# A two-layer hybrid block: the opening's loads, modulation and weight splits rearranged, with 18 unread matmuls on TensorE

## The chip, the core and the metric

The kernel runs on one core of one Trainium2 chip. The metric is the device time of one execution in microseconds (us). A core has five instruction streams that run side by side and wait for each other by semaphores: TensorE (PE in the profile; its weight loads are PEld), VectorE (DVE), ScalarE (ACT), GpSimd (POOL) and SyncE (SP). Each stream is strictly in order: an instruction that waits holds up everything behind it on its engine. In this kernel every load is issued by SP, so all loads stand in one queue.

## What is computed

Two layers of a flow-matching backbone act on 256 latent tokens (`x`) and 256 context tokens (`ctx`), 1024 features each, all in float32. Cut to the part that matters here, a layer begins like this:

```python
mod = (silu(c) @ w_mod[l] + b_mod[l])[:, None, :]
sh1, sc1, gt1, sh2, sc2, gt2 = split(mod, 6, axis=-1)
h = rms_norm(x, g_norm1[l]) * (1 + sc1) + sh1     # the same for ctx with c_ctx
z = h @ w_in[l]
...                                               # conv, Fourier, attention, gates, MLP
```

`z` feeds three mixers: a gated short convolution (columns B, C and X of `w_in`), a Fourier mixing (columns F) and attention (columns Q, K and V). Then come gates, projections and an MLP.

## The kernel before, in words

**Tiling.** Activations are kept feature-major: 8 feature tiles of 128 features, each with 512 tokens (two streams of 256). A product in near-float32 accuracy is three matmuls on split operands: high weight by high activation (L416), low weight by high activation (L419), high weight by low activation (L421). A weight chunk of 1024 rows by 256 columns is loaded as a raw tile; a "split" makes its high part by a cast on ScalarE (L356) and its low part by a subtraction on VectorE or GpSimd (L357).

**The opening** is all that stands before the first layer's other products. It needs `x` and `ctx` (1 MiB each; xraw), the shift and scale columns of `w_mod` (16 loads of 512 KiB, two for each feature tile; tiles `big`), and three chunks of `w_in` (F, C and X, each in two halves of 512 KiB: rows 0 to 511 for feature tiles 0 to 3, rows 512 to 1023 for tiles 4 to 7). Its steps:

- `turn_x` (L480, L484) transposes `x` on TensorE and copies it to xT; `spread_rows` gives 1/rms of each token to every partition.
- For each feature tile kt, `mod_start` multiplies the silu vector by that tile's shift and scale columns (L245, 16 matmuls that the trace records as 32), copies the sums (L252, DVE), transposes them (L254, PE) and adds the bias (L258, L262, DVE). `gain` is L231.
- `modulate` makes the normed tile: L209 (DVE), its high part L214 (ACT), its low part L201 (DVE).
- `go(kt)` runs the 18 matmuls of that feature tile: 6 for each of the chunks F, C, X.

The loop goes over kt = 0 to 7 and runs a tile's mod_start and modulate while TensorE does the products of the tile before. The chunks are split in whole halves of 1024 columns. Four of the six low parts are made by GpSimd: F's and C's first halves, C's and X's second halves.

**What follows** in the program: the product with chunk B (`convL_mm`, its raw tile `convL_raw`), the two Fourier products, then queries, keys and values. The raw tiles come from a pool of two buffers. F's raw tile (both halves) is the first, C's the second, and `convL_raw` takes the first again; its load can be issued when all that reads F's raw tile is done.

**What sets the order.** Program order is not the order on an engine: a scheduler moves instructions where it expects an engine to be free, save those held with `keep_in_program_order`. So work written later can stand early. Such work here: the rotary tables for attention (L648, L652 to L654 on DVE), 14 short instructions on `gqk`, `ropec` and `ropes`, whose six small loads (L594 to L598) stand on SP behind all 16 loads of `w_mod`.

Code lines that matter, as they are before:

```python
start_raw = [raw_tile(), raw_tile()]                 # F and C: the raw pool's two buffers
first_w = [Chunk(r, True, e) for r, e in zip(start_raw, ((G, V), (G, G), (V, G)))]
...
bch = None if last else plain(w_in[l], 0, OFF_B).prep()   # convL_raw: the first buffer again
```

Of the kernel before, what the change touches and what calls it, by code (L numbers as in the profile page):

```python
# [39 lines left out]
def hybrid_block_kernel(  # L40
# [197 lines left out]
    def mod_start(ft, parts, meanwhile):  # L238
        """Shift and scale of one feature tile, the sums over even and odd k side by side."""
        pb = pmod.tile([P, 2, P], F32, tag="mod", name=nm("mod"))  # L240
        ps, tp = pb[:, 0, :], pb[:, 1, :]
        for kt in range(KT):
            for i in range(2):
                g = 2 * i + kt % 2
                mm = PE.matmul(  # L245
                    ps[32 * g : 32 * g + 32, :], cT[:, kt, :], parts[:, i, kt, :],
                    start=kt < 2, stop=kt >= KT - 2,
                )
                if ft and kt == 0 and i == 0:
                    tc.keep_in_program_order(mm)  # L250
        sb = scratch()[:, :P]
        V.tensor_copy(sb, ps)  # L252
# [1 line left out]
        tc.keep_in_program_order(PE.transpose(tp, sb, ident))  # L254
        tv = tp.rearrange("p (g s) -> p g s", s=32)
        for i in (1, 0):
            m = modT[0][:, i * 8 + ft, :]
            V.tensor_tensor(  # L258
                m, tv[:, 2 * i, 0:2], prm[0][:, i * 8 + ft : i * 8 + ft + 1].to_broadcast([P, 2]),
                op=ALU.add,  # L260
            )
# [115 lines left out]

    def fetch(loads, nkt=8, eng=(V, V)):
        r = raw_tile()
        for dst, src in loads(r.rearrange("p (k n) -> p k n", n=256)):  # L380
            nc.sync.dma_start(dst, src)
# [60 lines left out]
    def start_mod(q):  # L442
        t = bigt([P, 2, 2, KT, P], F32)
        for f in range(2):
            for i in (1, 0):
                c0 = i * D + (2 * q + f) * P
                nc.sync.dma_start(  # L447
                    t[:, f, i], w_mod[0, :, c0 : c0 + P].rearrange("(k p) n -> p k n", p=P)
                )
                if (q, f, i) == (0, 0, 0):  # L450
                    start_weights(0)
        return t
# [38 lines left out]
    for l in range(DEPTH):  # L491
# [18 lines left out]
        if l == 0:  # L510
# [5 lines left out]
            first_w[0].prep(0)  # L516

            def between(kt):
                if kt > 1:
                    go(kt - 1, 0, 1)  # L520
                if kt == KT // 2:
                    first_w[1].prep(1)

            for kt in range(KT):
                mod_start(kt, sc0[kt // 2][:, kt % 2], lambda: between(kt))
                gn = gain(0, 1, 48, gn, kt, 1)
                modulate(hh, hl, [(kt, 0), (kt, 1)], rb, gn, sh1)
                if kt == 0:
                    for w in first_w[1:]:
                        w.prep(0)  # L530
# [1 line left out]
                    go(0, 0, 1)
                if kt:
                    go(kt - 1, 1, 3)
                if kt in (2, 4):
                    first_w[kt - 2].prep(1)
# [546 lines left out]
```

## Time and profile before

| | |
|---|---|
| time, median of 3 runs | 1157.92 us (1157.07 to 1158.3) |
| span of the profiled execution, first to last instruction | 1156.9 us |
| mean granted TensorE clock over the span | 0.997 |
| bytes read from HBM | 177.81 MB |

The profiled execution has no time of its own on the page beside its span; the timed runs lie 0.2 to 1.4 us above that span, so about 1 us lies around it.

How to read the rows below: the timeline gives start, duration, engine, line, operation, output<-inputs with shapes, the count of merged instructions, and in brackets the idle time of the engine just before, with what ended it. A `SPq` row is SP issuing a load, not the load itself. The table by windows gives for each stretch its length, then busy time and instruction count of each engine, the granted TensorE clock, the busy share of the DMA engines (it can exceed 1) and GB/s.

### The profile page before, as it was taken

The numbers are of one execution on the slowest core, as the hardware profiler recorded it, in microseconds if no ns is written. First come the engines' busy times: TensorE is split into PE (matmuls) and PEld (weight loads), VectorE is DVE, ScalarE is ACT, GpSimd is POOL, SyncE is SP. The second block draws the span as 40 slices with busy tenths as digits, with TensorE's granted clock in tenths as the row PEclk, the third lists the DMA queues.
The fourth block names the chain that finished last, engine by engine and source line by source line (L and its number), as shares of the span: only waits on it lengthen the run. The fifth ranks groups of instructions, "written<-read, shape, count | busy, mean of one in ns | idle before, by whom it ended". The sixth has DMA issues, their size and how long they took to land.

```text
span 1156.9 us, 18548 instructions
## 1 busy us (share of the span) xinstructions
PE 1134.0 (98%) x7451; PEld 1001.1 (87%) x7451; DVE 781.5 (68%) x1446; ACT 501.3 (43%) x890; POOL 59.3 (5%) x57
## 2 busy tenths in 40 slices
PE   6899999999999999999999999999999999999998
PEld 4689987887787998878888888899999999999998
DVE  4677775567879785776746664678876567755754
ACT  4244444434332454144234135244666456744641
POOL 2102100000000100000000000043300000000000
PEclk9999999999999999999999999999999999999999
DMA  9923222234656253555455664515434465555552
GB/s 289 288 80 107 92 91 92 83 90 120 192 167 189 77 175 129 185 181 180 134 176 199 212 211 150 188 63 182 129 129 127 123 209 172 197 183 176 189 187 81
DMA packets 165743, 180.06 MB, mean 156 GB/s; under 512 B 5245, under 2 KB 144153, under 8 KB 165657
## 3 DMA queue, kind: packets, MB, share of 16 engines
q1 hardware_dynamic: 165656, 178.88, 49.1%
q8 instruction: 58, 0.95, 0.3%
q14 instruction: 29, 0.23, 0.1%
HBM read 177.81 MB, written 1.05 MB: 155 GB/s over the span
## 4 chain that ended last, share of the span: by engine, by line
PE 90%; SPq 3%; DMA 3%; DVE 2%; ACT 1%; POOL 0%; issue 0%; DVEq 0%; ACTq 0%
PE ffL_mm L416 15%; PE ffL_mm L419 14%; PE ffL_mm L421 14%; PE gateL_mm L416 5%; PE gateL_mm L419 5%; PE gateL_mm L421 5%; PE agL_mm L416 3%; PE agL_mm L419 3%; PE agL_mm L421 3%; SPq L447 2%; PE woL_mm L419 2%; PE woL_mm L421 2%; PE woL_mm L416 2%; PE gateL_aux L796 2%; PE gateL_aux L771 2%; PE qkvL_mm L748 2%
## 5 line engine op out<-in xcount | busy, mean ns | idle before, releaser
L356 ACT CAST ffL_whi<-ffL_raw 128x1024 fp32r<-128x1024 f32 x128 | 134.2, 1050 | 223.5 <-PE ffL_mm L421 211.4
L357 DVE TENSOR_TENSOR ffL_wlo<-ffL_raw,ffL_whi 128x1024 fp32r<-128x1024 f32 x127 | 155.2, 1223 | 102.7 <-ACT ffL_whi L356 102.6
L416 PE MATMUL ffL_mm<-ffL_big,ffL_whi 128*128 128x256 f32 (+1 forms) x544 | 173.3, 329 | 0.3 <-DVE xT L434 0.3
L419 PE MATMUL ffL_mm<-ffL_big,ffL_wlo 128*128 128x256 f32 (+1 forms) x544 | 172.3, 327 | 0.0
L416 PE MATMUL ffL_mm<-woL_big,ffL_whi 128*128 128x258 f32 (+2 forms) x544 | 171.2, 328 | 0.0
L419 PE MATMUL ffL_mm<-woL_big,ffL_wlo 128*128 128x258 f32 (+2 forms) x544 | 170.8, 327 | 0.0
L421 PE MATMUL ffL_mm<-ffL_big,ffL_whi 128*128 128x256 f32 (+1 forms) x544 | 137.9, 327 | 0.0
L421 PE MATMUL ffL_mm<-woL_big,ffL_whi 128*128 128x258 f32 (+2 forms) x544 | 134.0, 328 | 0.0
L416 PEld LDWEIGHTS ffL_mm<-ffL_big,ffL_whi 128*128 128x128 f32 x544 | 103.4, 190 | 11.0 <-issue 2.5
L416 PEld LDWEIGHTS ffL_mm<-woL_big,ffL_whi 128*128 128x128 f32 x544 | 102.7, 189 | 10.2 <-issue 1.6
L419 PEld LDWEIGHTS ffL_mm<-ffL_big,ffL_wlo 128*128 128x128 f32 x544 | 103.4, 190 | 9.0 <-issue 0.4
L419 PEld LDWEIGHTS ffL_mm<-woL_big,ffL_wlo 128*128 128x128 f32 x544 | 102.9, 190 | 8.9 <-issue 0.4
L323 DVE SCALAR_TENSOR_TENSOR ffL_acc<-ffL_modr,cs,ffL_acc 128x512 f32<-128x512 f32 x126 | 90.4, 747 | 25.9 <-DMA ffL_modr<-in_w_mod_dram 24.8
L421 PEld LDWEIGHTS ffL_mm<-ffL_big,ffL_whi 128*128 128x128 f32 x544 | 93.6, 190 | 8.6
L421 PEld LDWEIGHTS ffL_mm<-woL_big,ffL_whi 128*128 128x128 f32 x544 | 91.2, 189 | 8.7
L357 DVE TENSOR_TENSOR gateL_wlo<-gateL_raw,gateL_whi 128x1024 fp32r<-128x1024 f32 x40 | 48.9, 1222 | 13.4 <-ACT gateL_whi L356 13.3
L356 ACT CAST gateL_whi<-gateL_raw 128x1024 fp32r<-128x1024 f32 x40 | 42.0, 1050 | 26.9 <-PE gateL_mm L421 20.7
L774 DVE TENSOR_REDUCE gateL_mx<-gateL_aux 128x1 f32<-128x512 f32 (+1 forms) x48 | 28.7, 600 | 34.5 <-PE gateL_aux L771 34.2
L434 DVE SCALAR_TENSOR_TENSOR xT<-ffL_mm,modT,xT 128x256 f32<-128x256 f32 x80 | 34.1, 478 | 25.3 <-PE ffL_mm L421 25.2
L416 PE MATMUL gateL_mm<-n1L_big,gateL_whi 128*128 128x512 f32 x128 | 50.8, 398 | 0.0
L419 PE MATMUL gateL_mm<-n1L_big,gateL_wlo 128*128 128x512 f32 x128 | 50.8, 397 | 0.0
L419 PE MATMUL woL_mm<-agL_big,woL_wlo 128*128 128x256 f32 (+1 forms) x160 | 47.4, 307 | 0.0
(325 smaller groups left out, 2447.6 us busy)
## 6 DMA issues: line engine op xcount, KB each, us to landing
ffL_raw<-in_w_ff_dram SPq DMA_DIRECT2D x64, 1024.0 KB, 5.2
ffL_modr<-in_w_mod_dram SPq DMA_DIRECT2D x53, 512.0 KB, 5.6
gateL_raw<-in_w_in_dram SPq DMA_DIRECT2D x16, 1024.0 KB, 7.1
init_big<-in_w_mod_dram SPq DMA_DIRECT2D x16, 512.0 KB, 7.6
agL_raw<-in_w_in_dram SPq DMA_DIRECT2D x8, 1024.0 KB, 5.2
woL_raw<-in_w_o_dram SPq DMA_DIRECT2D x8, 1024.0 KB
qkvL_raw<-in_w_in_dram SPq DMA_DIRECT2D x6, 1024.0 KB
agL_modr<-in_w_mod_dram SPq DMA_DIRECT2D x11, 512.0 KB, 3.6
```

Source lines behind the costliest of these rows:

```text
L323: v = V.scalar_tensor_tensor(a, r[:, kk, :], w, a, op0=ALU.mult, op1=ALU.add)
L356: a = A.copy(hi[:, :n], src)
L357: b = eng.tensor_tensor(lo[:, :n], src, hi[:, :n].bitcast(F32), op=ALU.subtract)
L416: m = PE.matmul(d, wh, rh, start=kt == first, stop=False)
L419: PE.matmul(d, wl, rh, start=False, stop=False)
L421: PE.matmul(d, wh, rl, start=False, stop=kt == final)
L434: V.scalar_tensor_tensor(xT[:, f, cs], ps[:, cs], gt[:, f, s : s + 1], xT[:, f, cs], op0=ALU.mult, op1=ALU.add,)
L447: nc.sync.dma_start(t[:, f, i], w_mod[0, :, c0 : c0 + P].rearrange("(k p) n -> p k n", p=P))
L748: PE.matmul(ps, a, wh, start=kt == 0, stop=False)
L771: PE.matmul(sc, qT[:, h, q0 : q0 + P], kT[:, h // 4, e, ks], start=e == 0, stop=e == 1)
L774: V.reduce_max(mx, sc, axis=AX.X, negate=True)
L796: PE.matmul(yp[g * HD : (g + 1) * HD, :], vt[:, k0 + kk, g * HD : (g + 1) * HD], pts[g][:, kk, :], start=kk == 0, stop=kk == nk - 1,)
```

## The change

Five things are changed, all in the opening of layer 0.

1. **Loads.** The two loads of `w_mod` for feature tile 0 and the bias rows now stand ahead of `x` on SP; `x` and `ctx` come in four loads in place of two; the second halves of the `w_in` chunks come after tile 5's `w_mod` columns instead of after tile 3's.
2. **Tile 0's shift and scale** are computed ahead of the transposes of `x`.
3. **No split on GpSimd.** The low parts are made on VectorE, and each chunk is split in slices, one feature tile at a time (`Sliced.part`), so the raw tiles of F, C and X are read until the slice of tile 7 is made.
4. **Grouping.** Tiles 4 and 5 share one mod_start with 256 columns.
5. **18 unread matmuls** (`warm`): three times six matmuls of two constant tiles, before the first transposes, after the first transposes of `x`, and before the first products.

```diff
+W_INIT, W_X, W_RMS = 6, 6, 6
...
+    sc0 = [bigt([P, 2, 2, KT, P], F32)]
+    start_mod(sc0[0], 0)
+    load_rows(0)
     for i, src in enumerate((x[0], ctx_in[0])):
-        nc.sync.dma_start(xraw[:, i], src.rearrange("(t p) d -> p t d", p=P))
-    load_rows(0)
+        for tt in range(2):
+            nc.sync.dma_start(xraw[:, i, tt], src[tt * P : (tt + 1) * P, :])
...
+    def warm(n):
+        ps = pmod.tile([P, P], F32, tag="mod", name=nm("mod"))
+        for _ in range(n):
+            tc.keep_in_program_order(PE.matmul(ps, ones, ident, start=True, stop=True))
...
+    class Sliced(Chunk):
+        def part(self, k0, k1):
+            i = k0 // 4
+            if i not in self.pieces:
+                self.pieces[i] = [wpool.tile([P, 1024], F32R, tag=t, name=nm(t))
+                                  for t in ("whi", "wlo")]
+            hi, lo = self.pieces[i]
+            c = slice((k0 - 4 * i) * 256, (k1 - 4 * i) * 256)
+            tc.keep_in_program_order(A.copy(hi[:, c], self.raws[i][:, c]))
+            tc.keep_in_program_order(V.tensor_tensor(
+                lo[:, c], self.raws[i][:, c], hi[:, c].bitcast(F32), op=ALU.subtract))
...
-    first_w = [Chunk(r, True, e) for r, e in zip(start_raw, ((G, V), (G, G), (V, G)))]
+    start_weights(0)
+    for f in range(1, KT):
...
+        start_mod(sc0[f // 2], f)
+        if f == 5:
+            start_weights(1)
+    first_w = [Sliced(r) for r in start_raw]
+
+    mod_start(0, sc0[0][:, 0:1], lambda: None)
+    gn = gain(0, 1, 48, None, 0, 1)
...
+            groups = [(0,), (1,), (2,), (3,), (4, 5), (6,), (7,)]
+            due = []
+            for n, fts in enumerate(groups):
+                while len(due) > 1:
+                    go(due.pop(0))
...
+                if n == 1:
+                    go(0, 0, 2)
+                if n:
+                    mod_start(f0, sc0[f0 // 2][:, f0 % 2 : f0 % 2 + nf],
+                              lambda: n == 1 or go(due[0], 0, 1))
+                    gn = gain(0, 1, 48, gn, f0, nf)
+                else:
+                    first_w[0].part(0, 1)
+                modulate(hh, hl, [(f, s) for f in fts for s in range(2)], rb, gn, sh1)
+                for w in first_w[not n :]:
+                    w.part(f0, f0 + nf)
+                if n == 0:
+                    turn_x(range(NT0, KT))
+                else:
+                    go(due.pop(0), cut, 3)
+                due += fts
```

In the lists below a row is line, operation, output<-inputs (with buffer numbers) and size; line numbers are those of each kernel's own file, and the changed kernel's are higher: L201, L209, L252 and L357 are L220, L228, L270 and L410 there, L416, L419 and L421 are L451, L454 and L456.

**VectorE, where the rotary tables stand.** Before, they follow the low part of feature tile 5 (L201), and the next copy for a mod_start (L252, tile 6) stands among them:

```order
L201 SCALAR_TENSOR_TENSOR n1L_big_189<-n1L_scr_473,modT_120,n1L_big_188 128x256
L648 TENSOR_SCALAR gqk<-gqk 128x64
L652 TENSOR_TENSOR qkvL_tc_118_885<-ropec,gqk 128x64
L653 TENSOR_TENSOR qkvL_ts_119_886<-ropes,gqk 128x32
L652 TENSOR_TENSOR qkvL_tc_116_877<-ropec,gqk 128x64
L653 TENSOR_TENSOR qkvL_ts_117_878<-ropes,gqk 128x32
L654 TENSOR_TENSOR qkvL_ts_117_878<-ropes,gqk 128x32
L252 COPY n1L_scr_511<-n1L_mod_494 128x128
```

After, on the same engine: the tables (L682 and L686 to L688) stand among the low parts of tiles 4 and 5, and ahead of all three slices of F, C and X for these tiles (L410; `n1L_wlo_521` is F's). Nine more of the table rows, like those shown, stand where the line of dots is.

```order
L228 SCALAR_TENSOR_TENSOR n1L_scr_515<-xT,init_gain_186,init_aux_221 128x256
L682 TENSOR_SCALAR gqk<-gqk 128x64
L686 TENSOR_TENSOR qkvL_tc_119_914<-ropec,gqk 128x64
L687 TENSOR_TENSOR qkvL_ts_120_915<-ropes,gqk 128x32
L688 TENSOR_TENSOR qkvL_ts_120_915<-ropes,gqk 128x32
L220 SCALAR_TENSOR_TENSOR n1L_big_238<-n1L_scr_511,modT_132,n1L_big_237 128x256
...
L688 TENSOR_TENSOR qkvL_ts_118_907<-ropes,gqk 128x32
L220 SCALAR_TENSOR_TENSOR n1L_big_238<-n1L_scr_515,modT_132,n1L_big_237 128x256
L410 TENSOR_TENSOR n1L_wlo_521<-init_raw_135,n1L_whi_520 128x512
L410 TENSOR_TENSOR n1L_wlo_525<-init_raw_136,n1L_whi_524 128x512
L410 TENSOR_TENSOR n1L_wlo_529<-init_modr_138,n1L_whi_528 128x512
```

What moved: before, all low weights of these tiles were made elsewhere or earlier, and a copy for mod_start waited behind the tables; after, the low weights of tiles 4 and 5 wait behind them.

**VectorE, at the opening's end.** After, the last reader of F's raw tile (`init_raw_135`) is the slice for tile 7, behind that tile's low parts:

```order
L228 SCALAR_TENSOR_TENSOR n1L_scr_653<-xT,init_gain_186,init_aux_221 128x256
L220 SCALAR_TENSOR_TENSOR n1L_big_238<-n1L_scr_650,modT_132,n1L_big_237 128x256
L220 SCALAR_TENSOR_TENSOR n1L_big_238<-n1L_scr_653,modT_132,n1L_big_237 128x256
L410 TENSOR_TENSOR n1L_wlo_521<-init_raw_135,n1L_whi_520 128x256
L410 TENSOR_TENSOR n1L_wlo_525<-init_raw_136,n1L_whi_524 128x256
L410 TENSOR_TENSOR n1L_wlo_529<-init_modr_138,n1L_whi_528 128x256
L464 TENSOR_TENSOR uL_big_694<-n1L_mm_239,uL_big_694 128x512
```

Before, the last VectorE reader of that tile (`init_raw_123` there) is the whole half for tiles 4 to 7, which stands behind tile 2's low parts and ahead of tile 3's copy:

```order
L201 SCALAR_TENSOR_TENSOR n1L_big_189<-n1L_scr_360,modT_120,n1L_big_188 128x256
L201 SCALAR_TENSOR_TENSOR n1L_big_189<-n1L_scr_363,modT_120,n1L_big_188 128x256
L357 TENSOR_TENSOR n1L_wlo_381<-init_raw_123,n1L_whi_380 128x1024
L252 COPY n1L_scr_401<-n1L_mod_384 128x128
L258 TENSOR_TENSOR modT_120<-n1L_mod_384,prm_110 128x2
```

What moved: the last read of F's raw tile goes from tile 2's place to tile 7's.

**SP, the load queue.** After (before, the rows from `ropec` to `convL_raw` stand in the same order, at the same place behind all sixteen loads of `w_mod`):

```order
L484 DMA init_raw_135<-in_w_in_dram 128x4x256
L484 DMA init_raw_136<-in_w_in_dram 128x4x256
L484 DMA init_modr_138<-in_w_in_dram 128x4x256
L115 DMA init_big_157<-in_w_mod_dram 128x8x128 x4
L628 DMA ropec<-in_rope_c_dram 128x2x64
L629 DMA ropes<-in_rope_s_dram 128x2x64
L631 DMA gqk<-in_g_q_dram 128x64
L632 DMA gqk<-in_g_k_dram 128x64
L631 DMA gqk<-in_g_q_dram 128x64
L632 DMA gqk<-in_g_k_dram 128x64
L291 DMA gateL_modr_1512<-in_w_mod_dram 128x2x512
L416 DMA convL_raw_737<-in_w_in_dram 128x8x256
```

What did not move: the tables' loads and `convL_raw`'s stay behind the same bytes. Further on, from the middle of layer 0's queries and keys to the end, the order on all engines is that of before, row by row.

More of the change, by code (lines that the diff above doesn't have):

```diff
@@ L109, in hybrid_block_kernel, with start_mod @@
     xraw = bigt([P, 2, 2, D], F32)
+    def start_mod(t, f):
+        for i in (1, 0):
+            c0 = i * D + f * P
+            nc.sync.dma_start(
+                t[:, f % 2, i], w_mod[0, :, c0 : c0 + P].rearrange("(k p) n -> p k n", p=P)
+            )
+    sc0 = [bigt([P, 2, 2, KT, P], F32)]
+    start_mod(sc0[0], 0)
+    load_rows(0)
     for i, src in enumerate((x[0], ctx_in[0])):
-        nc.sync.dma_start(xraw[:, i], src.rearrange("(t p) d -> p t d", p=P))
-    load_rows(0)
+        for tt in range(2):
+            nc.sync.dma_start(xraw[:, i, tt], src[tt * P : (tt + 1) * P, :])
     ident = const.tile([P, P], F32, tag="ident", name="ident")
@@ L122, in hybrid_block_kernel @@
     cs2 = const.tile([P, 2, KT], F32, tag="cs2", name="cs2")
+    def warm(n):
+        ps = pmod.tile([P, P], F32, tag="mod", name=nm("mod"))
+        for _ in range(n):
+            tc.keep_in_program_order(PE.matmul(ps, ones, ident, start=True, stop=True))
+    warm(W_INIT)
     prm = []
@@ L236, in gain, with mod_start @@
         return g
-    def mod_start(ft, parts, meanwhile):
-        pb = pmod.tile([P, 2, P], F32, tag="mod", name=nm("mod"))
-        ps, tp = pb[:, 0, :], pb[:, 1, :]
+    def mod_start(f0, parts, meanwhile):
+        n = parts.shape[1]
+        pb = pmod.tile([P, 2, n, P], F32, tag="mod", name=nm("mod"))
+        ps, tp = pb[:, 0], pb[:, 1]
         for kt in range(KT):
@@ L244, in mod_start @@
                 g = 2 * i + kt % 2
-                mm = PE.matmul(
-                    ps[32 * g : 32 * g + 32, :], cT[:, kt, :], parts[:, i, kt, :],
+                tc.keep_in_program_order(PE.matmul(
+                    ps[32 * g : 32 * g + 32], cT[:, kt, :], parts[:, :, i, kt, :],
                     start=kt < 2, stop=kt >= KT - 2,
[L248 to L252, printed above, removed]
+                ))
+        sb = scratch((P, 4, P))[:, :n]
+        tc.keep_in_program_order(V.tensor_copy(sb, ps))
         meanwhile()
-        tc.keep_in_program_order(PE.transpose(tp, sb, ident))
-        tv = tp.rearrange("p (g s) -> p g s", s=32)
+        for f in range(n):
+            tc.keep_in_program_order(PE.transpose(tp[:, f], sb[:, f], ident))
+        tv = tp.rearrange("p f (g s) -> p f g s", s=32)
         for i in (1, 0):
-            m = modT[0][:, i * 8 + ft, :]
-            V.tensor_tensor(
-                m, tv[:, 2 * i, 0:2], prm[0][:, i * 8 + ft : i * 8 + ft + 1].to_broadcast([P, 2]),
+            a = i * 8 + f0
+            m = modT[0][:, a : a + n, :]
+            tc.keep_in_program_order(V.tensor_tensor(
+                m, tv[:, :, 2 * i, 0:2], prm[0][:, a : a + n].unsqueeze(2).to_broadcast([P, n, 2]),
                 op=ALU.add,
-            )
-            V.tensor_tensor(m, tv[:, 2 * i + 1, 0:2], m, op=ALU.add)
+            ))
+            tc.keep_in_program_order(
+                V.tensor_tensor(m, tv[:, :, 2 * i + 1, 0:2], m, op=ALU.add))
     def mod_loads(todo):
@@ L439, in residual @@
                 acc[s].add(f)
[L442 to L452, printed above, removed]
     start_raw = [raw_tile(), raw_tile()]
@@ L464, in start_weights @@
             )
-    sc0 = [start_mod(0), start_mod(1)]
-    start_weights(1)
-    sc0 += [start_mod(2), start_mod(3)]
-    first_w = [Chunk(r, True, e) for r, e in zip(start_raw, ((G, V), (G, G), (V, G)))]
+    start_weights(0)
+    for f in range(1, KT):
+        if f % 2 == 0:
+            sc0.append(bigt([P, 2, 2, KT, P], F32))
+        start_mod(sc0[f // 2], f)
[4 more added lines that the diff above has]
+    gn = gain(0, 1, 48, None, 0, 1)
     ss0 = small([P, 4], "ss")
@@ L486, in hybrid_block_kernel @@
     turn_x(range(NT0))
+    warm(W_X)
     rb0 = spread_rows(ss0, 4)
+    warm(W_RMS)
     rb = [rb0[:, s * S : (s + 1) * S] for s in range(2)]
@@ L502, in hybrid_block_kernel @@
             hh, hl = bigt([P, KT, 512]), bigt([P, KT, 512])
-            gn = None
         else:
@@ L514, in go @@
                 fm(first_w[a:b], hsrc, (0, T), banks[2 * a : 2 * b], (kt,), 0, 7, True)
[L516 to L530, printed above, removed]
-                    turn_x(range(NT0, KT))
[L532 to L536, printed above, removed]
+            groups = [(0,), (1,), (2,), (3,), (4, 5), (6,), (7,)]
[3 more added lines that the diff above has]
+                    go(due.pop(0))
+                f0, nf = fts[0], len(fts)
+                cut = 2 if n == 1 else 1
+                if n == 1:
[10 more added lines that the diff above has]
+                if n == 0:
+                    turn_x(range(NT0, KT))
+                else:
+                    go(due.pop(0), cut, 3)
+                due += fts
             for i in range(3):
```

1 line of the change is left out of this document (added).

## The prediction

> **What bounds the kernel now.** First the page, then the table by windows, cut at TensorE's restarts.
>
> ```profile
> span 1156.9 us, 18548 instructions
> PE 1134.0 (98%) x7451; PEld 1001.1 (87%) x7451; DVE 781.5 (68%) x1446; ACT 501.3 (43%) x890; POOL 59.3 (5%) x57
> ```
>
> ```profile
> core 0: us, PE busy (x) PEld busy (x) DVE busy (x) ACT busy (x) POOL busy (x), PEclk, DMA share, GB/s
> 0.00:20.19 20.19, 9.47 (x75) 8.06 (x75) 7.50 (x24) 10.01 (x18) 4.63 (x12) 1.00 0.93 286
> 4.00:44.00 40.00, 32.52 (x278) 25.50 (x278) 21.15 (x62) 16.00 (x28) 7.05 (x4) 0.96 1.11 314
> 20.19:23.05 2.86, 2.86 (x6) 1.83 (x6) 1.46 (x3) 1.83 (x2) 1.90 (x1) 0.50 1.16 291
> 46.48:50.37 3.89, 0.74 (x3) 0.31 (x4) 2.53 (x10) 0.00 (x0) 1.14 (x1) 1.00 0.71 159
> 50.37:54.97 4.60, 4.60 (x14) 3.37 (x14) 3.03 (x17) 0.91 (x2) 0.00 (x0) 0.63 1.03 348
> 54.97:69.89 14.92, 14.92 (x122) 11.91 (x122) 8.32 (x24) 5.62 (x10) 0.27 (x4) 1.00 0.17 61
> 69.89:110.00 40.11, 40.11 (x294) 38.16 (x293) 30.26 (x74) 18.37 (x39) 4.87 (x6) 1.00 0.41 133
> 110.00:1150.00 1040.00, 1035.22 (x6687) 917.50 (x6686) 711.74 (x1257) 457.87 (x810) 42.27 (x33) 1.00 0.48 152
> ```
>
> TensorE is the bound from 54.97 on: no idle time to 110, and 4.78 us of it in the 1040 us after. So what the opening gains or loses reaches the end nearly one for one, and the change has to be read in the first 70 us. There TensorE starts products at 20.19 (at a granted clock of 0.50), stands still for 3.15 of the 3.89 us after 46.48, and runs at 0.63 behind that. The DMA engines are full from 4 to 44 us. What ends the middle stall is in the timeline:
>
> ```profile
> 42.70 2.41 POOL L357 TENSOR_TENSOR n1L_wlo<-init_raw,n1L_whi 128x1024 fp32r<-128x1024 f32 x1 [19.18 <-ACT n1L_whi L356]
> 43.27 4.63 DVE L201 SCALAR_TENSOR_TENSOR n1L_big<-n1L_scr,modT,n1L_big 128x256 fp32r<-128x256 f32 x2 [0.19 <-ACT n1L_big L214]
> ...
> 45.19 0.47 SPq L597 DMA_DIRECT2D gqk<-in_g_q_dram  x1
> ...
> 49.26 0.20 DVE L648 TENSOR_SCALAR gqk<-gqk 128x64 f32<-128x64 f32 x1 [1.36 <-DMA gqk<-in_g_q_dram]
> ...
> 50.03 0.28 DVE L252 COPY n1L_scr<-n1L_mod 128x128 f32<-128x128 f32 x1
> 50.23 0.21 DVE L652 TENSOR_TENSOR qkvL_tc<-ropec,gqk 128x64 f32<-128x64 f32 x1
> ...
> 50.37 0.33 PE L254 MATMUL n1L_mod<-ident,n1L_scr 128*128 128x128 f32 x1 [1.68 <-DVE n1L_scr L252]
> ...
> 51.11 0.15 DVE L258 TENSOR_TENSOR modT<-n1L_mod,prm 128x2 f32<-128x2 f32 x1
> ```
>
> Two things delay VectorE here. Two low parts (L201) take 4.63 us while GpSimd splits weights; then the rotary tables wait for `gqk`, whose load SP issues only at 45.19, behind the sixteen `w_mod` loads. The second ends last: 49.26 us, which I call T.
>
> **The change, part by part.**
>
> *Start.* Tile 0's shift and scale leave the path behind `x`, warm matmuls run in TensorE's idle time (the first window has 10.72 us of it), and GpSimd's splits go. All that can bring: the slow clock of the first six products (2.86 us at half clock, so 1.4), perhaps 1 us of an earlier start (x lands later by the 1 MiB put ahead of it, but the chain behind it is shorter; bounds minus 1 to plus 2), and 3.75 us of VectorE (4.63 against 0.88 for two L201 without GpSimd, row below). None of it reaches the end, since TensorE then runs into the next wait sooner: it would finish tile 3's products near 43, and VectorE reach the tables near 44 (20.2 less 1, less 1.4 of slow clock, plus four tiles of 5.5 us, and 2 for the doubled mod_start).
>
> The rule on this: the Trainium skill, TensorE: Matmul & The Clock Gate, "What's actually happening", says that half clock is the default after an idle window of about 3.4 us and full clock returns after about as much work. By it the warm matmuls save the 1.4 us, and a wait of less than 3.4 us further on costs no clock, which would make my sum below 1.2 us smaller (1164.8). The trace is harsher: idle stretches of 1.48 and 1.68 us with 0.74 us of work between were followed by a clock of 0.63.
>
> *The tables' wait.* The order on VectorE puts the tables ahead of all three low slices of tiles 4 and 5, without which `go(4)` stops at its second matmul. Their loads stand behind the same bytes as before, and the loads fill the DMA engines (314 GB/s from 4 to 44), so T stays 49.26 (bounds: minus 1 if the pieces of `x` flow better, plus 1 if `w_mod` at the head starts the flow later). Prices:
>
> ```profile
> 32.33 0.88 DVE L201 SCALAR_TENSOR_TENSOR n1L_big<-n1L_scr,modT,n1L_big 128x256 fp32r<-128x256 f32 x2 [0.19 <-ACT n1L_big L214]
> 33.67 1.23 DVE L357 TENSOR_TENSOR n1L_wlo<-init_raw,n1L_whi 128x1024 fp32r<-128x1024 f32 x1 [0.46 <-ACT n1L_whi L356]
> ...
> 54.97 1.08 PE L245 MATMUL n1L_mod<-init_big,init_scr 128*32 128x128 f32 x32
> ...
> 60.46 1.08 PE L245 MATMUL n1L_mod<-init_big,init_scr 128*32 128x128 f32 x32
> ...
> 64.92 0.89 DVE L201 SCALAR_TENSOR_TENSOR n1L_big<-n1L_scr,modT,n1L_big 128x256 fp32r<-128x256 f32 x2 [0.19 <-ACT n1L_big L214]
> ...
> 65.81 0.39 PE L416 MATMUL n1L_mm<-n1L_big,n1L_whi 128*128 128x512 f32 x1
> ...
> 69.89 0.39 PE L416 MATMUL convL_mm<-n1L_big,convL_whi 128*128 128x512 f32 x1
> 70.93 0.42 DVE L357 TENSOR_TENSOR fouL_wlo<-fouL_raw,fouL_whi 128x256 fp32r<-128x256 f32 x1
> ```
>
> After T, VectorE does 14 table rows (before: 49.26 to 51.11 with one L252 of 0.20 from start to start among them, so 1.65), two L220 (0.88) and F's slice of 512 columns (between 0.42 for 256 and 1.23 for 1024: 0.69). TensorE restarts at 49.26 + 3.22 = **52.5**, where it restarted at 50.37. Left then: 17 matmuls of `go(4)` (18 take 65.81 to 69.89, 4.08, so 3.9), plus 1.7 of slow clock (in 50.37 to 54.97 it lost 37% of 4.60), to mod_start(6) at 58.1; one tile period (54.97 to 60.46, 5.49) to mod_start(7) at 63.6; and as before 9.43 from there (60.46 to 69.89). The opening ends at 73.0 against 69.89: **plus 3.1**.
>
> *The load of `convL_raw`.* Before, F's raw tile was free after 33.67, and the load was issued long before use. Now its last reader is the slice of tile 7.
>
> ```profile
> 48.53 0.38 SPq L381 DMA_DIRECT2D convL_raw<-in_w_in_dram  x1
> ...
> 56.39 1.05 ACT L356 CAST convL_whi<-convL_raw 128x1024 fp32r<-128x1024 f32 x1 [3.28 <-DMA convL_raw<-in_w_in_dram]
> ...
> 70.45 0.37 SPq L381 DMA_DIRECT2D qkvL_raw<-in_w_in_dram  x1
> ...
> 75.92 1.05 ACT L356 CAST qkvL_whi<-qkvL_raw 128x1024 fp32r<-128x1024 f32 x1 [4.53 <-DMA qkvL_raw<-in_w_in_dram]
> 77.01 1.23 DVE L357 TENSOR_TENSOR qkvL_wlo<-qkvL_raw,qkvL_whi 128x1024 fp32r<-128x1024 f32 x1 [0.28 <-ACT qkvL_whi L356]
> ```
>
> Tile 7's low parts end 5.35 us after its L245 (65.81 less 60.46); with F's slice (0.42) the buffer is free at 63.6 + 5.8 = 69.4. SP is idle then and issues. The price of such a load in an empty queue is `qkvL_raw`'s: cast 5.47 after the issue, high part ready at 6.5, low part at 7.79 (78.24 less 70.45). So the high part is there at 75.95 and the low part at 77.2, while TensorE is done at 73.0. Behind the waiting load on SP stand `fouL_raw`, a `modr` load and layer 1's rows; TensorE needs none of them for another 5 us. Two matmuls run on the high part alone (0.45), so the stretch counts as started at 76.75; after 2.95 us idle the clock is slow again, as behind the 3.15 us before. It lasts some 3.6 us, of which 2.4 fall behind 77.2, and costs 1.2. The product with B stands where it would after a start at 77.95: 4.95 behind the opening's end. Bounds: the waiting load lands up to 1 us sooner or later, and the clock costs 0 to 1.8; 2.8 to 6.5.
>
> *Sum.* 77.95 less 69.89 is plus 8.06. The profiled execution goes from 1156.9 to 1165.0 in span; with about 1 us around it, as the runs have (median 1157.92), **1166.0 us**. Later slices, SP's order and GpSimd's other splits are as before, so nothing gives it back beyond part of the 4.78 us of idle time after 110.
>
> **The rivals.**
>
> *The B load is hidden* (its buffer is free earlier than I read, or the load is quicker than 3 us): only the 3.1 is left, 1161.0. For it: the buffers are given out by a pool that I read in the code, not in a trace. Against it: the load writes the whole raw tile, and the order shows a reader of that tile at tile 7.
>
> *The queue runs faster*, the one mechanism that ends on the other side. Place: SP's loads ahead of `gqk` and `convL_raw`. If the tables land before VectorE reaches them near 44, the restart is at 44 + 3.2 and the 8.1 falls by 5.3; if the 1 MiB load also takes 3 us in place of 5.47, it falls by 2.5 more, to plus 0.3: 1158.2. It decides when T is under 44 and the load under 5. Against it: 314 GB/s with full engines over 40 us, and the same bytes ahead of the tables (13.6 MB for the 13 MiB of `x`, `w_mod` and `w_in`: 43 us at that rate, from about 3.5).
>
> *GpSimd was the bound*: if the 4.63 us row made the whole stall, its end returns 3.15 idle and 1.7 of slow clock: 1153.0. For it: the first idle stretch, 1.48 us, is ended by that L201. Against it: behind it, VectorE still waits 1.36 us for `gqk`, and new work stands behind that wait. The Trainium skill, SBUF — State Buffer, "Who interferes with whom", says that a VectorE instruction with two SBUF inputs contends with a GpSimd instruction that reads SBUF; by that rule the removal frees VectorE at once. The trace agrees (4.63 against 0.88), but the rule says nothing of the wait behind it.
>
> *Later still*: T moves by 1 or more, or the conv and Fourier stretch finds another late load: 1169.
>
> That the change does not do what it says (warm matmuls that leave the clock at half) would cost 1.4 us ahead of the tables' wait and change nothing behind it.
>
> **How the numbers follow.** Forecast 0.72 (1166.0, own range 1163.5 to 1168); B load hidden 0.10 (1161.0); faster queue 0.06 (1158.2); GpSimd 0.06 (1153.0); later 0.06 (1169). The measurement can tell about 0.2% here, 2.3 us. Faster 0.06; same 0.06; slower 0.88. The range takes the forecast and the hidden load and leaves out both lower cases and most of the later one: 1160.5 to 1168.5.
>
> **What would show it.** In the profile after: VectorE idle until `gqk` near 49 with TensorE idle from about 43 to 52.5; products at half clock behind; no GpSimd split in the opening and two low parts in 0.9 us; SP idle until near 69, then `convL_raw`; TensorE idle for about 3 us ahead of the first `convL_mm`, near 76, and a first pause behind its first two matmuls. Wrong, if the tables start without a wait, or `convL_raw` is issued near 48 as before.

## The result and the profile after

| | before | after |
|---|---|---|
| time, median | 1157.57 us (1157.07 to 1158.3) | 1165.36 us (1164.99 to 1166.6) |
| ratio | | 1.0073, 95% interval 1.0061 to 1.0085 (the two medians alone give 1.0067) |
| span of the profiled execution | 1156.9 us | 1163.7 us (its time: 1165.53) |

The changed kernel is slower by 0.7%. The table by windows of the kernel after, cut at TensorE's restarts as it was for before (length, then busy time and count for each engine, granted TensorE clock, DMA share, GB/s):

```profile
0.00:19.81 19.81, 14.62 (x111) 13.46 (x111) 6.78 (x25) 9.71 (x18) 2.28 (x11) 1.00 0.94 295
19.81:22.76 2.95, 2.95 (x12) 2.17 (x12) 1.14 (x4) 0.55 (x2) 0.00 (x0) 1.00 1.14 288
45.90:52.10 6.20, 0.00 (x1) 0.01 (x1) 3.19 (x18) 0.49 (x1) 0.00 (x0) 0.69 0.52 144
52.10:57.60 5.50, 5.50 (x17) 4.19 (x17) 1.15 (x2) 0.00 (x0) 0.00 (x0) 0.73 0.01 3
57.60:72.79 15.19, 15.19 (x121) 11.65 (x120) 8.50 (x28) 5.79 (x14) 0.27 (x4) 1.00 0.20 61
72.79:83.05 10.26, 7.48 (x20) 5.46 (x20) 8.64 (x12) 3.25 (x4) 0.00 (x0) 0.67 0.76 251
110.00:1150.00 1040.00, 1036.85 (x6706) 919.31 (x6706) 717.87 (x1274) 462.71 (x824) 44.68 (x35) 1.00 0.48 152
```

The start is better than before: products begin at 19.81 at full clock (before: at 20.19, at half clock), and GpSimd (the fifth pair) splits nothing. Then TensorE stands still for 6.20 us ahead of 52.10, and for 2.78 of the 10.26 us behind 72.79, with a slow clock after both. In the long stretch from 110 on it idles 3.15 us (before: 4.78).

The timeline of the kernel after at the first of these places:

```profile
45.41 0.49 PE L451 MATMUL n1L_mm<-n1L_big,n1L_whi 128*128 128x512 f32 x1 [1.69 <-ACT n1L_whi L409]
48.83 0.20 DVE L682 TENSOR_SCALAR gqk<-gqk 128x64 f32<-128x64 f32 x1 [4.53 <-DMA gqk<-in_g_q_dram]
51.36 1.28 DVE L410 TENSOR_TENSOR n1L_wlo<-init_raw,n1L_whi 128x512 fp32r<-128x512 f32 x2
52.10 0.80 PE L454 MATMUL n1L_mm<-n1L_big,n1L_wlo 128*128 128x512 f32 x1 [6.20 <-DVE n1L_wlo L410]
57.60 1.08 PE L265 MATMUL n1L_mod<-init_big,init_scr 128*32 128x128 f32 x32
63.04 1.08 PE L265 MATMUL n1L_mod<-init_big,init_scr 128*32 128x128 f32 x32
```

VectorE is ready at 44.3 and stands 4.53 us at a row of the rotary tables that TensorE does not need for a long time yet; behind it in the queue is F's low slice (L410), for which TensorE stands 6.20. The first table row begins at 48.83, where it began at 49.26 before: the loads came only 0.4 us sooner, and VectorE came earlier to wait for them.

And at the second place, with SP's queue:

```profile
46.73 0.38 SPq L291 DMA_DIRECT2D gateL_modr<-in_w_mod_dram  x1
68.75 0.38 SPq L416 DMA_DIRECT2D convL_raw<-in_w_in_dram  x1
...
74.01 1.99 ACT L377 CAST convL_whi<-convL_raw 128x1024 fp32r<-128x1024 f32 x2 [1.49 <-DMA convL_raw<-in_w_in_dram]
75.11 0.83 PE L451 MATMUL convL_mm<-n1L_big,convL_whi 128*128 128x512 f32 x2 [2.17 <-ACT convL_whi L377]
76.55 1.22 PE L454 MATMUL convL_mm<-n1L_big,convL_wlo 128*128 128x512 f32 x2 [0.61 <-DVE convL_wlo L378]
...
82.26 0.48 PE L454 MATMUL convL_mm<-n1L_big,convL_wlo 128*128 128x512 f32 x1
83.05 0.40 PE L451 MATMUL convL_mm<-n1L_big,convL_whi 128*128 128x512 f32 x1
```

SP issues nothing for 22 us, then `convL_raw`, 20.2 us later than before (48.53). The cast follows 5.26 us after the issue, and TensorE waits twice: 2.17 us for the high part and 0.61 for the low part. Its matmuls then take 0.43 us each instead of 0.23 until 82.4.

### The profile page after: what moved, and what is told of

Same layout as the page of the kernel before. It is cut to its first block, busy times and chain, and to the rows that moved or that the text cites. A ratio compares the mean times of both kernels' runs of the same rounds, so it can differ in the third digit from the quotient of the medians.

```text
span 1163.7 us, 18582 instructions
## 1 busy us (share of the span) xinstructions
PE 1140.6 (98%) x7455; PEld 1006.4 (86%) x7455; DVE 780.7 (67%) x1459; ACT 502.7 (43%) x905; POOL 49.3 (4%) x53
## 4 chain that ended last, share of the span: by engine, by line
PE 92%; SPq 3%; DMA 2%; DVE 1%; issue 0%; POOL 0%; ACT 0%; DVEq 0%; ACTq 0%
PE ffL_mm L451 15%; PE ffL_mm L456 15%; PE ffL_mm L454 15%; PE gateL_mm L454 5%; PE gateL_mm L451 5%; PE gateL_mm L456 5%; PE agL_mm L451 3%; PE agL_mm L454 3%; PE agL_mm L456 3%; SPq L115 3%; PE woL_mm L454 2%; PE woL_mm L456 2%; PE woL_mm L451 2%; PE gateL_aux L830 2%; PE gateL_aux L805 2%; PE qkvL_mm L783 2%
## 5 line engine op out<-in xcount | busy, mean ns | idle before, releaser
L451 PE MATMUL ffL_mm<-ffL_big,ffL_whi 128*128 128x256 f32 (+1 forms) x544 | 173.3, 329 | 0.0
L454 PE MATMUL ffL_mm<-ffL_big,ffL_wlo 128*128 128x256 f32 (+1 forms) x544 | 172.3, 327 | 0.0
L451 PE MATMUL ffL_mm<-woL_big,ffL_whi 128*128 128x258 f32 (+2 forms) x544 | 171.0, 328 | 0.0
L454 PE MATMUL ffL_mm<-woL_big,ffL_wlo 128*128 128x258 f32 (+2 forms) x544 | 170.7, 327 | 0.0
L456 PE MATMUL ffL_mm<-ffL_big,ffL_whi 128*128 128x256 f32 (+1 forms) x544 | 138.0, 327 | 0.0
L456 PE MATMUL ffL_mm<-woL_big,ffL_whi 128*128 128x258 f32 (+2 forms) x544 | 133.9, 328 | 0.0
L451 PEld LDWEIGHTS ffL_mm<-ffL_big,ffL_whi 128*128 128x128 f32 x544 | 103.4, 190 | 10.6 <-issue 2.1
L451 PEld LDWEIGHTS ffL_mm<-woL_big,ffL_whi 128*128 128x128 f32 x544 | 103.0, 190 | 10.2 <-issue 1.6
L454 PEld LDWEIGHTS ffL_mm<-ffL_big,ffL_wlo 128*128 128x128 f32 x544 | 103.5, 190 | 9.1 <-issue 0.4
L454 PEld LDWEIGHTS ffL_mm<-woL_big,ffL_wlo 128*128 128x128 f32 x544 | 103.1, 190 | 8.9 <-issue 0.4
L456 PEld LDWEIGHTS ffL_mm<-ffL_big,ffL_whi 128*128 128x128 f32 x544 | 93.7, 190 | 8.7
L456 PEld LDWEIGHTS ffL_mm<-woL_big,ffL_whi 128*128 128x128 f32 x544 | 91.2, 190 | 8.7
L451 PE MATMUL gateL_mm<-n1L_big,gateL_whi 128*128 128x512 f32 x128 | 50.8, 398 | 0.0
L454 PE MATMUL gateL_mm<-n1L_big,gateL_wlo 128*128 128x512 f32 x128 | 50.8, 397 | 0.0
L454 PE MATMUL woL_mm<-agL_big,woL_wlo 128*128 128x256 f32 (+1 forms) x160 | 47.4, 307 | 0.0
```

What stands on the lines that cost most here:

```text
L451: m = PE.matmul(d, wh, rh, start=kt == first, stop=False)
L454: PE.matmul(d, wl, rh, start=False, stop=False)
L456: PE.matmul(d, wh, rl, start=False, stop=kt == final)
```

## The experiments

Each kernel was timed beside the kernel before on the same chip; the ratios are against that. The kernel before had medians of 1156.5 to 1157.1 us there, so the medians of two rows from different chips compare to about 0.6 us.

| kernel | median, us | ratio to before (95%) |
|---|---|---|
| e1: after, tables' loads early | 1160.82 | 1.0037 (1.0024 to 1.0050) |
| e2: after, F's half cut whole | 1160.76 | 1.0035 (1.0022 to 1.0048) |
| e3: both | 1158.20 | 1.0012 (1.0002 to 1.0021) |
| e4: after, no warm matmuls | 1168.10 | 1.0100 (1.0083 to 1.0117) |
| e5: after, tables on GpSimd | 1158.62 | 1.0016 (1.0007 to 1.0025) |
| e6: e5, F's half whole, convL's cuts late | 1155.15 | 0.9985 (0.9976 to 0.9994) |
| e7: e6, no warm matmuls | 1154.97 | 0.9980 (0.9971 to 0.9990) |
| b1: before, low parts on VectorE | 1158.85 | 1.0020 (1.0010 to 1.0030) |
| b2: before, tables on GpSimd | 1156.47 | 0.9998 (0.9988 to 1.0007) |
| b3: b1 and b2 | 1159.03 | 1.0020 (1.0010 to 1.0030) |
| b4: b3, convL's cuts late | 1152.21 | 0.9962 (0.9949 to 0.9974) |
| e8: e6, F's half cut earlier | 1151.47 | 0.9956 (0.9942 to 0.9969) |

### e1 to e3: one wait away, the other, both

```diff
 # e1: the tables' six loads, in the loop that loads w_mod
         if f == 5:
             start_weights(1)
+            nc.sync.dma_start(ropec, ...)
...
 # e2: F's second half in one cut, so that its raw tile is free with tiles 4 and 5
-                for w in first_w[not n :]:
-                    w.part(f0, f0 + nf)
+                    if w is not first_w[0] or f0 < 4:
+                        w.part(f0, f0 + nf)
+                    elif f0 == 4:
+                        w.part(4, 8)
```

> The changed kernel (1165.4 us) with the six loads of the rotary tables issued on SP ahead of the last four w_mod loads instead of behind them. Theory (two waits): VectorE reached the table rows at 44.3 and stood until 48.83 for gqk; without that wait the low slice of F goes 4.5 earlier, TensorE's restart goes from 52.10 to about 47.6, the opening's end from 72.8 to 68.3, the issue of convL_raw from 68.75 to 64.3 with everything behind it, so 1165.4 - 4.5 = 1160.9 us, still slower than before. Rival (the added matmuls and VectorE's larger share cost the time, the waits are cover): at most 1 us better, 1164.5 to 1165.5. Rival (the weights' and w_mod loads bound tiles 4 to 7): w_mod lands 4 us later, restart early but mod_start(6) still near 57, 1165 or more.

> The changed kernel with the second half of F cut in one piece of 1024 columns with tiles 4 and 5 instead of 512, 256 and 256, so that F's raw tile is free near 52.6. Theory (two waits): convL_raw is issued near 52.7 instead of 68.75 and its product begins where the opening ends, 72.8, instead of as if at 78.96 (18 products done at 83.05, 0.23 each at full clock): 6.1 less, some of it lost to a low pass for convL that VectorE now runs ahead of tile 6's copy (up to 1.5): 1159.3 to 1161 us. The tables' wait stays at 48.83 and the restart near 52.6 to 52.8. Rival (the loads are hidden and the opening's other work costs the time): within 1 us of 1165.4.

> Both edits. Theory: the gains add, 1165.4 - 4.5 - 6.1 = 1154.8 us, 2 to 3 us faster than before (1157.6); up to 1.5 more if VectorE's low pass for convL stands ahead of tile 6's copy, and about 1.5 more if the wait of 1.4 us that the changed kernel lost near layer 0's feed-forward comes back: 1154.8 to 1158. Rival (one wait takes the place of the other): no better than the better of the two alone, 1159 to 1161.

e1 and e2 each took about 4.5 us off, which is what was expected, but e1 not by the expected path. Its timeline:

```profile
42.03 0.20 DVE L682 TENSOR_SCALAR gqk<-gqk 128x64 f32<-128x64 f32 x1 [4.50 <-DMA gqk<-in_g_q_dram]
44.29 0.69 PE L273 MATMUL n1L_mod<-ident,n1L_scr 128*128 128x128 f32 x2 [3.34 <-DVE n1L_scr L270]
50.16 0.50 PE L454 MATMUL n1L_mm<-n1L_big,n1L_wlo 128*128 128x512 f32 x1 [0.23 <-DVE n1L_wlo L410]
54.24 1.08 PE L265 MATMUL n1L_mod<-init_big,init_scr 128*32 128x128 f32 x32
```

With earlier loads the scheduler also puts the table rows earlier, now ahead of the copy of tiles 4 and 5, and VectorE waits 4.50 us there. TensorE waits 3.34 us for that copy, and the matmul that restarted at 52.10 in the kernel after comes at 50.16, not at 47.6; mod_start(6) comes 3.4 us earlier (54.24 against 57.60). The profiled execution was the fastest of the five (1159.66, 5.9 us below that of the kernel after). The rest of its gain is the clock, which stayed full behind the convL wait, where it was half for 6.83 us in the kernel after (last section).

In e2 the second wait is gone:

```profile
52.47 0.38 SPq L416 DMA_DIRECT2D convL_raw<-in_w_in_dram  x1
...
52.50 0.80 PE L454 MATMUL n1L_mm<-n1L_big,n1L_wlo 128*128 128x512 f32 x1 [6.02 <-DVE n1L_wlo L410]
59.45 1.08 PE L265 MATMUL n1L_mod<-init_big,init_scr 128*32 128x128 f32 x32
74.32 0.39 PE L451 MATMUL convL_mm<-n1L_big,convL_whi 128*128 128x512 f32 x1
```

The load goes out at 52.47 and the product with B begins without a wait. The 4.5 us are what each edit gave, not what each cause costs: e1 moved its wait and did not end it, and in e2 the clock stayed at half until 58.70, where it was full again from 55.12 in the kernel after. e3 is 2.6 us below either alone, just outside the range of the theory: the tables' wait had moved ahead (3.05 us of TensorE), and VectorE's low pass for convL stood ahead of tile 6's copy, 5.25 us for its load. Those two waits are what e5 and e6 take away.

### e4: without the 18 matmuls

```diff
-W_INIT, W_X, W_RMS = 6, 6, 6
+W_INIT, W_X, W_RMS = 0, 0, 0
```

> The changed kernel without the 18 matmuls without a reader. Theory: the first products run at half clock again, about 1.4 us later for TensorE, but VectorE still stands at the tables until 48.83, so the restart stays at 52.1 and the time at 1165.4, within 0.5. Rival (the warm matmuls hold up the opening's transposes and cost the time): 2 us or more faster. Rival (they save what they were put in for): 1.4 us or more slower.

A miss: 2.7 us slower, and not for the rival's reason.

```profile
19.12 0.50 PE L451 MATMUL n1L_mm<-n1L_big,n1L_whi 128*128 128x512 f32 x1 [1.51 <-ACT n1L_big L233]
49.46 0.20 DVE L682 TENSOR_SCALAR gqk<-gqk 128x64 f32<-128x64 f32 x1 [7.49 <-DMA gqk<-in_g_q_dram]
53.51 0.80 PE L451 MATMUL n1L_mm<-n1L_big,n1L_whi 128*128 128x512 f32 x1 [10.29 <-ACT n1L_whi L409]
```

The first product begins earlier (19.12) and at full speed. The loss comes at the tables: the scheduler, whose times had shifted, put the table rows ahead of two multiplications of tiles 4 and 5. VectorE waits 7.49 us, TensorE 10.29. So this run says nothing on the worth of the warm matmuls; e7 asks that again.

### e5 to e8: the waits taken away cleanly

The table rows go to GpSimd, which has nothing else to do there, so they can block nobody.

```diff
 # e5, both layers
-            V.tensor_scalar(gg, gg, f, None, op0=ALU.mult)
+            G.tensor_scalar(gg, gg, f, None, op0=ALU.mult)
...
 # e6: e5, the edit of e2, and convL's chunk ahead of the last products
+            bch = plain(w_in[0], 0, OFF_B)
+            bch.pin = True
+            bch.prep()
             for i in range(3):
                 go(KT - 1, i, i + 1)
...
 # e8: e6, with F's second half cut behind tile 3's slices
+                if f0 == 3:
+                    first_w[0].part(4, 8)
```

> The changed kernel with the rotary tables' small multiplications of both layers on GpSimd instead of VectorE; their loads stay where they are. VectorE then has no table row to stand at. Theory (two waits): VectorE goes on at 44.3, F's low slice starts when ScalarE's cast is there (45.4), TensorE's restart goes from 52.10 to about 46.1, without the slow stretch behind the 6.2 us wait: 6 to 7.3 less up to mod_start(6), and everything behind it, convL_raw's wait unchanged: 1158.1 to 1159.4 us. Rival (the loads of w_mod for tiles 6 and 7 bound): mod_start(6) not before 54 and a gain of at most 3.5: 1162. Rival (tables were cover for something else that ends as late): 1164 or more.

> The edit before, plus F's second half cut whole with tiles 4 and 5, plus convL's load and cuts written ahead of the last products and held in that order, so that VectorE's low pass for convL no longer stands ahead of tile 6's copy. Theory (the two waits are the whole loss, and the opening's gain comes out when both are gone): 6.1 less than the edit before, 1152 to 1153.5 us; up to 2 more if the feed-forward's wait of 1.4 us comes back: 1152 to 1155.5, in any case faster than before. Rival (the opening's new form has a cost of its own): 1157 or more.

> The same kernel without the 18 matmuls without a reader. In the run without them alone the first product began at 19.12 instead of 19.81, already at 0.23 us a matmul, so the theory is now that they buy no clock and hold the opening up: 0.5 to 0.8 us less than with them. Rival (they save a slow start, as the prediction had it): 1.4 us more than with them.

> The kernel with both waits removed (1155.15), with the cut of F's second half moved from behind tile 5's modulation to behind tile 3's slices. Theory (what bounds the opening now is the wait of 2.1 us for ScalarE's cast and 0.8 us for F's low pass at tile 4): VectorE and ScalarE are idle there, F's half has landed (issued at 30.7, 6.6 us to land), so 1.5 to 2.9 us less: 1152.3 to 1153.7 us, faster than the kernel before by 0.25 to 0.4 per cent. Rival (F's half has not landed then and the cut holds up tile 4's modulation): 1155 or more.

e5, timeline:

```profile
45.50 0.50 PE L451 MATMUL n1L_mm<-n1L_big,n1L_whi 128*128 128x512 f32 x1 [1.70 <-ACT n1L_whi L409]
46.22 0.50 PE L454 MATMUL n1L_mm<-n1L_big,n1L_wlo 128*128 128x512 f32 x1 [0.23 <-DVE n1L_wlo L410]
50.30 1.08 PE L265 MATMUL n1L_mod<-init_big,init_scr 128*32 128x128 f32 x32
67.76 0.73 PE L451 MATMUL convL_mm<-n1L_big,convL_whi 128*128 128x512 f32 x2 [2.10 <-ACT convL_whi L377]
```

The wait of 6.20 is 0.23, mod_start(6) comes 7.3 us earlier as expected, and the convL wait stands unchanged behind it. The median falls by 6.7. e6 takes that one too and is 0.15% faster than before, at the upper end of its range. What is left, against e8:

```profile
46.03 0.50 PE L451 MATMUL n1L_mm<-n1L_big,n1L_whi 128*128 128x512 f32 x1 [2.12 <-ACT n1L_whi L409]
47.29 0.50 PE L454 MATMUL n1L_mm<-n1L_big,n1L_wlo 128*128 128x512 f32 x1 [0.76 <-DVE n1L_wlo L410]
52.98 1.08 PE L265 MATMUL n1L_mod<-init_big,init_scr 128*32 128x128 f32 x32
```

```profile
45.34 0.50 PE L451 MATMUL n1L_mm<-n1L_big,n1L_whi 128*128 128x512 f32 x1 [0.36 <-ACT n1L_whi L409]
46.06 0.50 PE L454 MATMUL n1L_mm<-n1L_big,n1L_wlo 128*128 128x512 f32 x1 [0.22 <-DVE n1L_wlo L410]
48.80 1.08 PE L265 MATMUL n1L_mod<-init_big,init_scr 128*32 128x128 f32 x32
63.67 0.39 PE L451 MATMUL convL_mm<-n1L_big,n1L_whi 128*128 128x512 f32 x1
```

In e6 (first fence) the waits at tile 4 are 2.12 and 0.76 us, where e5, with the smaller cut, had 1.70 and 0.23 and no slow clock behind them; in e6 the clock is half from 48.56 to 51.98. In e8 (second) the cut is made where ScalarE and VectorE stood idle: mod_start(6) comes 4.2 us earlier, the product with B begins at 63.67 (69.89 before), and the time is 1151.47, 0.44% under the kernel before (0.31 to 0.58). That is 0.8 us better than the expected range; the granted clock is 1.00 over the whole span of e8, so the slow stretch went with the waits. e7 equals e6 within the measurement (0.2 us apart): neither its theory nor the rival holds.

### b1 to b4: the same on the kernel before

```diff
 # b1
-    first_w = [Chunk(r, True, e) for r, e in zip(start_raw, ((G, V), (G, G), (V, G)))]
+    first_w = [Chunk(r, True, e) for r, e in zip(start_raw, ((V, V), (V, V), (V, V)))]
 # b2: the table rows on GpSimd, as in e5; b3: both; b4: b3 with convL's chunk as in e6
```

> The kernel before with the opening's four low passes on VectorE instead of GpSimd, nothing else. Theory (the tables' wait swallows what GpSimd gives back): VectorE's slowed pair (4.63 us) goes to 0.9, but it stands at the tables until about 49.26 all the same and has two low passes of 1.2 behind or ahead of them: restart 50.4 to 52, 1157 to 1159 us, no gain. Rival (GpSimd was the bound): 3.7 less, 1153.3 us.

> The kernel before with the rotary tables' multiplications on GpSimd, nothing else. Theory (the kernel before stood at the same tables, less long): VectorE comes free of its slowed pair at 47.9 and takes tile 4's copy there instead of at 50.03, TensorE's restart goes from 50.37 to about 48.3: 2.1 less, 1155 us. Rival (this wait was hidden in the kernel before): 1157.1, no change.

> The kernel before with both: low passes on VectorE, tables on GpSimd. Theory: what GpSimd gave back comes out once the tables no longer stand in the way: VectorE's pair near 45.5, tile 4's copy near 46.6, restart near 47, 3.4 less: 1153.6 us, up to 1.3 more if the two early low passes on VectorE put the first product off: 1153.5 to 1155. Rival (low passes on VectorE cost what they save): 1155 to 1157.

> The kernel before with low passes on VectorE and tables on GpSimd (1159.0), with convL's load and cuts written ahead of the last products and held in that order. Theory (there VectorE's low pass for convL stood 6.0 us ahead of tile 6's gain and TensorE 3.8 us ahead of tile 7's sums): these 3.8 and the slow stretch behind them go, 1153.5 to 1155 us. Rival (the low passes on VectorE are what made that kernel slow): 1157 or more.

b1 tests the rival of the prediction by which GpSimd was the bound:

```profile
43.11 0.87 DVE L201 SCALAR_TENSOR_TENSOR n1L_big<-n1L_scr,modT,n1L_big 128x256 fp32r<-128x256 f32 x2
49.07 0.20 DVE L648 TENSOR_SCALAR gqk<-gqk 128x64 f32<-128x64 f32 x1 [5.08 <-DMA gqk<-in_g_q_dram]
```

The pair L201 falls from 4.63 to 0.87 us, and VectorE then waits 5.08 us for `gqk` where it waited 1.36. The time is 0.2% worse. b2 and b3 missed: without the tables' wait they should have gained 2 to 3 us. b2 gained nothing and b3 lost 0.2%. b3, VectorE and TensorE:

```profile
56.45 1.23 DVE L357 TENSOR_TENSOR convL_wlo<-convL_raw,convL_whi 128x1024 fp32r<-128x1024 f32 x1 [6.02 <-ACT convL_whi L356]
58.30 1.35 PE L245 MATMUL n1L_mod<-init_big,init_scr 128*32 128x128 f32 x32 [3.78 <-issue]
```

A third wait of the same kind had taken the place: the low pass for convL, put by the scheduler ahead of tile 6's gain, waits 6.02 us for its load, and TensorE 3.78 behind it (in b2 4.82 and 2.58). b4 holds that pass back behind tile 7's modulation and is 6.8 us faster than b3 by the medians, 5.5 by the spans of the profiled executions (1154.7 and 1149.2): mod_start(7) comes at 54.25 instead of 58.30, and the slow clock that b3 had from 58.97 to 62.38 is gone.

## Why the prediction was right

Term by term, as the prediction put them:

| step | predicted | measured |
|---|---|---|
| tile 3's products done | near 43 | 43.7 |
| VectorE at the tables | near 44 | 44.3 |
| tables begin (T) | 49.26 | 48.83 |
| TensorE's restart | 52.5 | 52.10 |
| slow clock behind it, cost | 1.7 | 1.5 |
| mod_start(6), mod_start(7) | 58.1, 63.6 | 57.60, 63.04 |
| opening ends | 73.0 | 72.79 |
| `convL_raw` issued | 69.4 | 68.75 |
| high part, low part there | 75.95, 77.2 | 75.1, 76.5 |
| slow clock behind the low part, cost | 1.2 | 2.9 |
| product with B stands as after a start at | 77.95 (+8.06) | 78.96 (+9.07) |

The measured 78.96 is the time at which 18 matmuls of convL are done (83.05) less the 4.08 that 18 took at full clock.

**The start's gains swallowed by the next wait.** Right within its bounds (0.4 us earlier, where about 1 was counted; full clock; L220 pairs of 0.9) and in effect: nothing of it was left at 52.10. That the tables' wait is what swallows it is shown by e5, where taking the table rows off VectorE returned 6.7 us, and from the other side by b1.

**The tables' wait.** Right, in the wait, in what stood behind it and in the cost of the slow clock: TensorE ran at half from 52.10 to 55.12, which costs 1.5 us where 1.7 was counted.

**The load of `convL_raw`.** Right in its mechanism and shown by e2 and e6: with F's raw tile free near 52 (e2) or 48 (e6), the load goes out there and the wait is gone. One size was off: the slow clock behind it. The prediction counted 3.6 us of it, costing 1.2 behind the low part; the clock was half from 75.60 to 82.42 and cost 2.9 (78.96 less 76.55, plus the two matmuls' 0.45).

**The carry to the end.** "Nearly one for one" fits better than the spans say. Of the +9.07 at the opening, 9.1 us are still there at the first `gateL_mm` matmul (137.03 against 127.90) and 7.3 at the last `ffL_acc` addition (774.77 against 767.48); the spans differ by 6.8. Most of what is missing is two waits of the kernel before between 740 and 770:

```profile
PE ffL_mod L280 <- DVE ffL_acc L323: 1.4, 1, 1.4
PE ffL_mm L416 <- DVE xT L434: 0.3, 1, 0.3
```

Both are absent after. But that is not a gain of the change: b1 to b4 run the code of the kernel before there, and in their profiles the first wait is 0 to 0.6 us, as in all others. So the profiled execution of the kernel before was a long one. Its span says the same: it lies only 0.7 us under the median time, while every execution on record that has both numbers has 1.7 to 3.0 us outside its span (the run after 1.8). The "about 1 us around it" ahead of the prediction came from a span and times of different executions. By the medians the change costs 7.8 us.

So the closeness of the sum (1166.0 against 1165.4) is in part luck, made of terms that cancel: clock +1.7 and the load and the opening's end -0.7 ahead of the product with B, -2.3 behind it (1.7 of it the two waits of a long profile before; the rest could not be placed), +0.8 outside the span.

**The rivals.** "The B load is hidden" is ruled out by the trace (issue at 68.75). "The queue runs faster": the tables landed 0.4 sooner, not 5. "GpSimd was the bound": b1 is 0.2% slower instead of 0.4% faster. "The warm matmuls leave the clock at half": the clock was full at 19.81. What they are worth in time is not settled. With them all seven profiled kernels kept full clock until tile 4 at least; of the seven without them, five (before, b1, b2, b4, e7) ran 3.41 us at half clock from near 20, and b3 and e4 did not. Yet the medians of e6 and e7 are equal, with e7's ten runs spread over 3.7 us and e6's over 1.6.

**What the change is worth.** With the waits removed on both sides, the new opening (e8) and the old one (b4) differ by 0.7 us with overlapping intervals, and in their profiles mod_start(7) begins at 54.24 and 54.25, the product with B at 63.67 and 63.69. The comparison is kind to the new one, since e8 also has a cut moved by hand and b4 has not. What the new opening has gained by mod_start(4) (36.79 against 37.88 in b4) is gone by mod_start(6) (48.80 against 48.79); why the tiles that share a mod_start take 1.1 us longer was not asked. The loss of 0.7% is thus not in the work that was added, but in two places where an instruction queue and a buffer turned early readiness into waiting. The low pass for convL, a third such place, shows in e3, b2 and b3.

## What to carry to other kernels

When a stretch is made faster, look at what stands next in each in-order queue behind it and when its data lands: an instruction that waits for a late load costs as much more as its engine arrives sooner. Cutting a weight in slices keeps its raw tile in use until the last slice, so ask which load waits for that buffer. After every edit read the new order on the engines, because the scheduler may move such instructions in front of others again, as it did in e1 and e4.

## What was not expected of the hardware

How long the clock stays slow differs behind waits that are alike. The clock that the traces record changes in steps: all half-clock stretches of the 14 profiles, but for the last ones that the end of the record cuts, last 3.41, 6.83, 10.24 or 13.65 us, one to four times 3.41, and within one profile they lie on one grid of that step. Behind the restart near 52 it was two steps in the kernel after (48.29 to 55.12, so it began during the wait) and three in e2 (48.46 to 58.70). Behind the pair of waits at convL, alike to 0.2 us, it was two steps after, one in e5 and none in e1. The table by windows, cut on the grid, shows what differs. First the kernel after, then e5, then e1 at that place, last e6 at tile 4:

```profile
72.18:75.60 3.42, 1.25 (x6) 0.59 (x4) 2.67 (x5) 1.93 (x3) 0.00 (x0) 1.00 1.07 378
75.60:79.01 3.41, 2.80 (x8) 2.00 (x7) 3.41 (x6) 1.66 (x3) 0.00 (x0) 0.50 0.24 81
79.01:82.42 3.41, 3.41 (x10) 2.67 (x9) 2.56 (x4) 0.00 (x0) 0.00 (x0) 0.50 0.96 298
65.39:68.81 3.42, 1.01 (x4) 0.30 (x2) 3.15 (x5) 2.15 (x3) 0.00 (x0) 1.00 1.07 382
68.81:72.22 3.41, 2.94 (x7) 2.37 (x8) 3.41 (x6) 1.10 (x2) 0.00 (x0) 0.50 0.21 40
67.51:70.92 3.41, 2.06 (x10) 1.37 (x8) 2.41 (x5) 1.48 (x4) 0.00 (x0) 1.00 1.08 378
70.92:74.33 3.41, 1.88 (x7) 1.26 (x8) 3.41 (x5) 3.06 (x4) 0.00 (x0) 1.00 0.70 245
45.15:48.56 3.41, 1.78 (x7) 1.24 (x8) 2.84 (x4) 1.86 (x3) 0.00 (x0) 1.00 0.74 182
```

In the kernel after and in e5 the longer wait falls whole into one step, TensorE is busy for 1.25 and 1.01 us of that step, and the next one runs at half. In e1 a boundary of the grid (70.92) cuts the longer wait in two, TensorE is busy for 2.06 and 1.88 us of the two steps, and the clock stays full. Over the 14 profiles, every full-clock step with TensorE busy for at most 0.50 of it was followed by half clock and none with 0.53 or more; between these, both came (e6, with 1.78 us: half). Full clock came back behind steps that were busy for 0.80 or more, though not behind all: the 0.82 of the kernel after (2.80 us, above) did not bring it back.

Where the grid lies against the work differs from one execution to the next: the first slow step begins at 20.15 in the kernel before, at 18.83 in b1 and at 19.80 in b2. So the same wait can cost nothing or, for each slow step, up to 1.7 us (half of 3.41). This fits the spread among runs of one kernel: of e7's ten, the three fastest (1153.1 to 1153.7 us) had a mean granted clock of 1.000 and the slowest (1156.8) 0.995, though no run set the grid on purpose. The warm matmuls act at the same place: in the step ahead of 20.15 TensorE was busy for 0.46 us in the kernel before, and in the kernel after for 3.0 us or more of every step from 17.57 to 41.46. The Trainium skill, TensorE: Matmul & The Clock Gate, "What's actually happening", says that the clock is set by activity windows of about 3.4 us that run freely. The traces agree in the steps of 3.41 us. The same place speaks of a whole idle window; here two waits of 2.1 and 0.8 us (e6) were enough for the slow clock.
